# Weights stand still in the output and down projections of an encoder block, and its second norm sums over partitions

## The chip, the cores and the metric

The kernel runs on one core of one Trainium2 chip. Its engines work side by side, each through its own queue in program order: TensorE (PE in the profile, its weight loads PEld), VectorE (DVE), ScalarE (ACT), GpSimd (POOL) and SyncE (SP), which issues most transfers. The metric is the device time of one execution in microseconds (us); all times below are in us unless marked ns.

## The reference

One layer over 1024 tokens of 1024 features, all in float32. What matters here is the part behind the mixers:

```
h = rms_norm(x, norm1_g);  z = h @ w_in          # 1024 x 2560
conv_out = conformer_conv(...)                   # 512 features
attn_out = neighbourhood_attention(...)          # 512 features
mix = concatenate([conv_out, attn_out])          # 1024 x 1024
x = x + mix @ w_out                              # output projection, 1024 x 1024
h = rms_norm(x, norm2_g)                         # mean of squares over the 1024 features
x = x + (silu(h @ w_gate) * (h @ w_up)) @ w_down # 1024 x 2816 twice, then 2816 x 1024
```

`rms_norm` divides each token by the root of the mean square of its features and multiplies by a gain per feature.

## The kernel before

**Products.** Every float32 operand is split into a high part (`hi`, rounded to the matmul's own float32 format) and the rest (`lo`). `mac` (L120) makes one step of a product of three matmuls, hi x hi, hi x lo and lo x hi, each with 128 rows in common, 128 stationary columns and up to 512 moving ones. `split` (L113) makes hi on ACT and lo on DVE or POOL. The three large products (output projection, gate/up, down) are done with seven block products instead of eight, on halves of rows, columns and the common dimension; sums and differences of the halves are the operands. "Half 0" and "half 1" of the tokens are the upper and the lower eight grid rows; each is cut into four column blocks of 128 tokens.

**Attention.** A loop over `i` (L898 to L937) runs 32 head pairs as a pipeline: scores, softmax, transposes of the weights (`flip`), weighted sums (`weigh`). After each block of four pairs `evac_hi` and `evac_lo` (L698 to L719) take the result out of PSUM: half 0 into `rowf`, half 1 into `a11` (hi and lo) and `diff` (half 1 less half 0). The order of the blocks is 0, 3, 1, 2, with half 0 before half 1. Weights of the next stage are split between (`take_parts`).

**Output projection.** The seven groups n1, n7, n4, n6, n5, n2, n3 (L1120 to L1141) each have four accumulators `pb[cb]` and four steps `c` for each. `proj` (L770) holds 128 tokens of the activations still (`lhs`) and moves 512 output features of the weights `wq` past them: the result is 128 tokens by 512 features. `fill` (L869) puts the four steps of n1's block 0 into the end of the attention loop. `read` (L874) adds each result into `x2[t]`, a tile of 128 tokens by 1024 features, on DVE (`put`, L863). Tokens 0 to 3 (half 0) are complete after n5, 4 to 7 (half 1) after n3.

**Second norm.** `norm2(t)` (L943) stores `x2[t]` to `xd` in DRAM for the last residual, sums its squares on ACT along the tile's rows and takes the root; `norm2_out(t)` (L950) scales by the reciprocal and by the gain `g2b`, which lies broadcast over all partitions. Gate/up needs features on partitions, so `turn(t, j)` (L1061) transposes four 128 x 128 blocks on TensorE into PSUM and copies them out with ACT: for half 0 as hi into `h2` and plain into `xT`, for half 1 plain into `xT`. That is 16 calls, 64 transposes.

**Operands of gate/up.** From the two halves `xT` come S1 to S4 (`s_sum`, L1023) and their splits (`s_split`, L1045). A11 and A12 are the parts of `h2`. The first products are m1 and m2 of row blocks 0 to 3, which need A11 and A12 only; then m6 (S2), m5 (S1), m7 (S3), m3 (S4) and m4 (A22), each for blocks 0 and 1, then for 2 and 3. `product` (L1166) runs four steps; `evac` (L1177) reads the bank; `prep` splits the weights four products ahead, on ACT and POOL.

**Order by hand.** All engines' queues follow program order. `weaves` (L1086) fills a list of small jobs, and each step of `proj` or `product` pops one: that puts transposes, norms, splits and conversions between the matmuls. The dictionary `plan` (L1143) does this for products 0 to 14. `x2`, `xn`, `xT`, weights and many others share 22 buffers of one size (`G`); PSUM banks are shared by tag (`mm` four, `tp` two, `cv`).

**Down projection.** `down` (L1358) holds 128 tokens of the hidden activations still and moves 512 features of `w_down`; `finish` adds the residual from `xd`, `store` writes rows of the output.

Of the kernel before, what the change touches and what calls it, by code (L numbers as in the profile page):

```python
# [31 lines left out]
def layout(v):  # L32
# [21 lines left out]
        "x": f["x"],  # L54
        "xt": f["x"].T.reshape(4, 2, P, 2, 512).transpose(3, 0, 2, 1, 4),
# [6 lines left out]
        "g2": f["norm2_g"][None],  # L62
# [12 lines left out]
def build(ctx, tc, a):  # L75
# [622 lines left out]
    def evac_hi(s_):  # L698
        rh, cb = order[s_]
        if rh == 0:  # L700
            if not rowf:
                rowf.extend(G(f"rf{j}").rearrange("p (c b q) -> p c b q", c=2, b=4) for j in range(2))
            for j in range(2):
                act.copy(rowf[j][:, :, cb], os_[s_][:, 2 * j:2 * j + 2])
        else:
            a11[cb] = [w.rearrange("p (c q) -> p c q", c=4) for w in lr(G(f"a11{cb}", F32R))]
            act.copy(a11[cb][0], os_[s_])

    def evac_lo(s_, js=(0, 1)):
        rh, cb = order[s_]  # L710
        if rh == 0:
            return
        if not diff:
            diff.extend(G(f"df{j}").rearrange("p (c b q) -> p c b q", c=2, b=4) for j in range(2))
        for j in js:
            cs = slice(2 * j, 2 * j + 2)
            hi, lo = [w[:, cs] for w in a11[cb]]
            dve.tensor_tensor(lo, os_[s_][:, cs], hi.bitcast(F32), OP.subtract)
            dve.tensor_tensor(diff[j][:, :, cb], os_[s_][:, cs], rowf[j][:, :, cb], OP.subtract)  # L719
# [38 lines left out]
    x2, xn, qop = {}, {}, {}  # L758

    def lhs(p, c, cb):  # L760
        if p == "n1":
            return [w[:, c] for w in a11[cb]]
        q, o = qop[LHS[p]], c * 512 + cb * P
        return [q[:, o:o + P], q[:, 2048 + o:2048 + o + P]]
# [3 lines left out]
    CB = (0, 3, 1, 2)  # L768

    def proj(p, cb, acc, cs=range(4), start=True):  # L770
# [81 lines left out]
    def rows(ap, t):  # L852
        rh, cb = divmod(t, 4)
        return ap.rearrange("(h i w) d -> h i w d", h=2, w=GW)[rh, :, cb * 16:cb * 16 + 16, :]

    def load_x2(t):
        x2[t] = G(f"x2{t}")
        nc.sync.dma_start(x2[t], rows(a["x"], t))

    def add_x(t):  # L860
        return lambda: pool.dma_start(x2[t], rows(a["x"], t), accum_op=OP.add)
# [7 lines left out]
    def fill(*cs):  # L869
        if 0 not in pb:  # L870
            pb[0] = mm("n10")
        proj("n1", 0, pb[0], cs)

    def read(p, cb):  # L874
        acc = pb[cb]
        if p == "n1":
            x2[4 + cb] = G(f"x2{4 + cb}")
            l, r = lr(x2[4 + cb])
            act.copy(l, acc)
            dve.tensor_scalar(r, acc, -1.0, None, op0=OP.mult)  # L880
        elif p == "n7":
            put(cb, 1, acc, OP.subtract)
            put(cb, 0, acc)
        elif p in ("n4", "n6"):
            put(cb, 0, acc, OP.add if p == "n4" else OP.subtract)
        elif p == "n5":
            put(cb, 1, acc)
            put(4 + cb, 1, acc)
            norm2(cb)
        elif p == "n2":  # L890
            put(4 + cb, 0, acc)
        else:
            put(4 + cb, 1, acc)
            norm2(4 + cb)
# [3 lines left out]
    for i in range(2, 32 + 2):  # L898
# [32 lines left out]
        if i > 2:  # L931
# [3 lines left out]
            elif i > 6 and i % 4 in (0, 3):  # L935
                evac_lo((i + 1) // 4 - 2, (0,) if i % 4 == 3 else (1,))
        if jobs:  # L937
            jobs.pop(0)()
    fill(3)

    sd2 = {}

    def norm2(t):  # L943
        nc.sync.dma_start(xd[t * P:(t + 1) * P, :], x2[t])
        ss = SM(f"s2{t}", 1)
        act.activation(cv(f"jk{t}"), x2[t], AF.Square, accum_out=ss)
        sd2[t] = SM(f"r2{t}d", 1)
        act.activation(sd2[t], ss, AF.Sqrt, bias=eps, scale=1.0 / D)

    def norm2_out(t):  # L950
        r = SM(f"r2{t}r", 1)
        dve.reciprocal(r, sd2[t])
        xn[t] = G(f"xn{t}")
        dve.scalar_tensor_tensor(xn[t], x2[t], r, g2b, OP.mult, OP.mult)
# [66 lines left out]
    sn, sop, xT = {}, {}, {}  # L1021

    def s_sum(t, ns, eng):  # L1023
        (x11, x12), (x21, x22) = lr(xT[t]), lr(xT[t + 4])
        for n in ns:
# [3 lines left out]
            if n == 4:  # L1029
                if not s4:  # L1030
                    s4.extend(G(f"s4{j}").rearrange("p (k s) -> p k s", s=512) for j in range(2))
                for j in range(2):
                    eng.tensor_tensor(s4[j][:, :, t * P:(t + 1) * P], *[w[:, j * 256:(j + 1) * 256].rearrange(
                        "p (k s) -> p k s", s=P) for w in (x12, s2)], OP.subtract)
                continue
            o, l, r = ((s1, x21, x22), (s2, x11, s1), (x21, x11, x21))[n - 1]
            eng.tensor_tensor(o, l, r, OP.subtract)

    s4 = []

    def s_rows(n, t):
        return {"S1": lambda: sn[t][:, :512], "S2": lambda: sn[t][:, 512:], "S3": lambda: xT[t + 4][:, :512],
                "A22": lambda: xT[t + 4][:, 512:]}[n]()

    def s_split(n, t, eng=dve):  # L1045
        if n == "S4":
            if t == 0:
                q = [lr(G(f"S4{i}", F32R)) for i in range(HK)]
                sop[n] = [[w[h] for w in q] for h in range(2)]
            split(sop[n][0][t], sop[n][1][t], s4[t // 2][:, t % 2], (eng,))  # L1050
            return
        if n not in sop:
            q = H(n, F32R).rearrange("p (w k s) -> p w k s", w=2, s=512)
            sop[n] = [[q[:, h, i] for i in range(HK)] for h in range(2)]
            sop[n, "all"] = [q[:, h] for h in range(2)]
        split(*[w[:, :, t * P:(t + 1) * P] for w in sop[n, "all"]],
              s_rows(n, t).rearrange("p (k s) -> p k s", s=P), (eng,))

    rest = []

    def turn(t, j):  # L1061
        if not h2:
            h2.extend(H(f"h2{w}", F32R).rearrange("p (k s) -> p k s", s=512) for w in range(2))
        pt = (tp, mm)[j](f"t2{t}{j}")
        for i in range(4):
            kb = 4 * j + i
            pe.transpose(pt[:, i * P:(i + 1) * P], xn[t][:, kb * P:(kb + 1) * P], ident)
        if j == 0:
            xT[t] = G(f"xT{t}")
        w = lr(xT[t])[j]  # L1070
        if t < 4:
            hi, lo = [q[:, 4 * j:4 * j + 4, t * P:(t + 1) * P] for q in h2]
            p3 = pt.rearrange("p (k s) -> p k s", s=P)
            act.copy(hi, p3)
            act.copy(w, pt)
            rest.append(lambda: dve.tensor_tensor(lo, p3, hi.bitcast(F32), OP.subtract))
        else:
            act.copy(w, pt)

    g2b = G("g2b")  # L1080
    nc.sync.dma_start(g2b, a["g2"].to_broadcast([P, D]))
# [16 lines left out]
    def N(t):  # L1098
        return lambda: norm2_out(t)

    def U(t, j):
        return lambda: turn(t, j)
# [7 lines left out]
    lo2 = lambda: rest.pop(0)()  # L1110

    def group(p, cbs=CB):
        for cb in cbs:
            more = p in ("n7", "n5")
            if not more:
                pb[cb] = mm(f"{p}{cb}")
            proj(p, cb, pb[cb], start=not more)
            read(p, cb)

    for cb in CB:  # L1120
        load_x2(cb)
    weaves(12, s0=lambda: (weigh(31), evac_hi(7), evac_lo(7)), s1=QS("Q3", diff, 0, pool), s2=lambda: tails.pop()(), s3=[lambda: read("n1", 0), add],
           s4=QS("Q3", diff, 1, pool), s6=C(0, 1), s10=take)
    group("n1", CB[1:])
# [6 lines left out]
    weaves(16, s1=take, s3=QS("Q4", diff, 1, pool), s6=take, s9=N(0), s13=N(3))  # L1131
# [3 lines left out]
    for _ in range(3):  # L1135
        next_raw()
    weaves(16, s0=take, s1=[N(1), U(0, 0)], s2=U(0, 1), s3=[lo2, lo2], s4=U(3, 0), s5=[U(3, 1), N(2)], s6=[lo2, lo2],
           s7=U(1, 0), s8=U(1, 1), s9=[lo2, lo2, prep], s10=[U(2, 0), take], s11=U(2, 1), s12=[lo2, lo2], s13=prep)
    group("n2")
    weaves(16, s3=prep, s7=prep, s9=N(4), s12=U(4, 0), s13=[U(4, 1), N(7)], s15=SS(0, 1, 2))  # L1140
# [3 lines left out]
        0: dict(s0=U(7, 0), s1=[U(7, 1), N(5)], s3=N(6)),  # L1144
        1: dict(s0=U(5, 0), s1=U(5, 1), s2=SP("S2", 0), s3=SS(3, 1, 2)),
        2: dict(s0=U(6, 0), s1=[U(6, 1), lambda: act.activation(warm, eps, AF.Silu)], s2=SS(1, 1, 2)),
        3: dict(s0=SP("S2", 3), s1=SS(2, 1, 2), s3=SP("S2", 1)),
        4: dict(s0=SP("S2", 2), s1=SP("S1", 0), s3=SP("S1", 3)),
        5: dict(s0=SP("S1", 1), s1=SP("S1", 2), s2=SS(0, 3), s3=SS(3, 3)),
        6: dict(s0=SS(1, 3), s1=SS(2, 3), s3=SP("S3", 0)),  # L1150
        7: dict(s1=SP("S3", 3), s2=SS(0, 4, eng=pool)),
        8: dict(s2=SS(3, 4, eng=pool)),
        9: dict(s1=SP("S3", 1), s3=SS(1, 4)),
        10: dict(s1=SP("S3", 2), s3=SS(2, 4)),
        11: dict(s1=SP("S4", 0), s3=SP("S4", 1)),
# [245 lines left out]
```

## Time and profile before

| what | value |
|---|---|
| median of 3 runs | 1050.73 (1049.7 to 1051.93) |
| the profiled execution, own time | 1050.14 |
| its span, first to last instruction | 1048.4 |
| mean granted TensorE clock | 0.999 of full |
| transposes of `turn`: 64, first and last start | 381.4 and 415.8 |
| first matmul of the gate/up products | 406.38 |
| output of the last block written from | 1041.39 on |

The profile lists instructions by engine with start and length. Matmuls are pipelined: their lengths overlap, so what a matmul costs is its spacing to the next, not its length. A stretch of the trace gives, for each engine, its busy time and its count of instructions; a wait names who ended it.

### The profile page before, as it was taken

To read this page: it belongs to the slowest core of one execution; us is meant where nothing else is said; L and a number is where in the kernel's file an instruction comes from. 1 tells how busy PE (TensorE), PEld (TensorE's weight loads), DVE (VectorE), ACT (ScalarE), POOL (GpSimd) and SP (SyncE) were. 2 spreads that over 40 slices of the span, in tenths; PEclk is the share of its full clock that TensorE was granted. 3 is DMA by queue.
4 is the path that set the end of the run, shared out by engine and by line. 5 is a ranking of instruction groups with operands and counts; after the bars stand their busy time and mean duration, and the time that the engine had idled before them with its cause. 6 is when DMAs were issued, how large, how long until landed. Compare 5 with 4: busy or idle time off the path is not lost.

```text
span 1048.4 us, 13903 instructions
## 1 busy us (share of the span) xinstructions
PE 1028.2 (98%) x4972; PEld 833.8 (80%) x4972; DVE 722.9 (69%) x1097; ACT 465.3 (44%) x915; POOL 452.6 (43%) x342
## 2 busy tenths in 40 slices
PE   7999999999999999999999999999999999999997
PEld 5888888776657888778888888888888888888885
DVE  6768998976896575876564655646556567768883
ACT  6466346636776676532232232232322443443441
POOL 0226578833575863655545454455454100002310
PEclk9999999999999999999999999999999999999999
DMA  9496771285536754465232132232232597633641
GB/s 334 178 271 220 225 238 61 77 244 168 148 109 163 159 182 141 109 167 174 104 131 101 71 131 101 89 132 93 99 111 81 207 326 256 205 101 125 215 133 40
DMA packets 74678, 162.93 MB, mean 155 GB/s; under 512 B 13489, under 2 KB 22193, under 8 KB 73905
## 3 DMA queue, kind: packets, MB, share of 16 engines
q1 hardware_dynamic: 67776, 144.14, 40.7%
q0 software_dynamic: 4864, 10.49, 5.9%
q10 hardware_dynamic: 1968, 7.42, 2.0%
q8 instruction: 39, 0.64, 0.2%
q14 instruction: 31, 0.25, 0.1%
HBM read 122.86 MB, written 53.15 MB: 168 GB/s over the span
## 4 chain that ended last, share of the span: by engine, by line
PE 88%; DVE 4%; POOL 2%; DMA 2%; ACT 2%; issue 2%; SPq 0%; POOLq 0%; ACTq 0%; DVEq 0%
PE B L122 5%; PE B L123 5%; PE B L124 5%; PE D L123 4%; PE D L124 4%; PE D L122 4%; PE A L122 3%; PE A L123 3%; PE A L124 3%; PE z L123 3%; PE z L122 3%; PE z L124 3%; PE gl L124 3%; PE gl L123 3%; PE gl L122 3%; PE n L122 3%
## 5 line engine op out<-in xcount | busy, mean ns | idle before, releaser
L347 DVE SCALAR_TENSOR_TENSOR cv<-u,par,cv 128x1009 f32<-128x1009 f32 (+14 forms) x85 | 108.5, 1276 | 2.0
L373 POOL TENSOR_TENSOR pa<-pa,pr 128x1022 f32<-128x1022 f32 (+10 forms) x31 | 75.2, 2426 | 33.7 <-ACT pr L372 32.2
L1356 POOL TENSOR_TENSOR ou<-ou,resm 128x512 f32<-128x512 f32 x8 | 12.5, 1571 | 142.5 <-DMA resm<-xd 142.5
L114 ACT CAST op<-sr 128x512 fp32r<-128x512 f32 x77 | 47.7, 619 | 52.7 <-PE B2d L124 21.3
L118 DVE TENSOR_TENSOR op<-sr,op 128x512 fp32r<-128x512 f32 x77 | 58.2, 756 | 16.4 <-ACT op L114 16.4
L1193 DVE TENSOR_TENSOR g<-B,g 128x512 f32<-128x512 f32 x22 | 15.2, 690 | 71.3 <-PE B L124 68.2
L1202 ACT ACTIVATE D<-D 128x512 f32<-128x512 f32 x22 | 12.8, 582 | 112.5 <-DVE D L1201 112.5
L1185 DVE TENSOR_TENSOR u<-B,g 128x512 f32<-128x512 f32 x22 | 15.2, 691 | 61.0 <-PE B L124 61.0
L668 POOL TENSOR_SCALAR e<-e,rs 128x288 f32<-128x288 f32 (+1 forms) x64 | 35.0, 568 | 45.6 <-DVE rs L666 41.0
L114 ACT CAST op<-wd 128x512 fp32r<-128x512 f32 x66 | 40.9, 620 | 30.4 <-DVE wd L1280 17.4
L118 DVE TENSOR_TENSOR op<-wd,op 128x512 fp32r<-128x512 f32 x66 | 50.5, 765 | 1.9 <-ACT op L114 0.3
L986 DVE TENSOR_TENSOR ts<-ts,gu 128x512 f32<-128x512 f32 x36 | 43.3, 1203 | 0.6
L1191 ACT ACTIVATE A<-A 128x512 f32<-128x512 f32 x18 | 10.5, 582 | 68.6 <-PE A L124 68.6
L661 ACT ACTIVATE e<-e,mx 128x288 f32<-128x288 f32 (+1 forms) x64 | 36.3, 569 | 2.9 <-DVE mx L659 2.8
L659 DVE CUSTOM_DVE_ANT_0 e<-s,tab 128x288 f32<-128x288 f32 (+1 forms) x64 | 29.7, 501 | 8.7 <-PE s L646 8.4
L372 ACT ACTIVATE pr<-u,par 128x1022 f32<-128x1022 f32 (+10 forms) x31 | 34.2, 1135 | 1.2 <-ACT vs L433 1.2
L677 PEld LDWEIGHTS p<-ident,e 128*96 128x96 f32 (+1 forms) x192 | 20.0, 133 | 18.1 <-POOL e L668 10.4
L677 PE MATMUL p<-ident,e 128*96 128x128 f32 (+1 forms) x192 | 28.5, 281 | 2.3 <-DVE pT L682 1.0
L986 DVE TENSOR_TENSOR ts<-gu 128x512 f32<-128x512 f32 x18 | 30.1, 1670 | 0.0
L865 DVE TENSOR_TENSOR x<-x,n 128x512 f32<-128x512 f32 x32 | 21.0, 681 | 13.1 <-PE n L124 13.1
L693 PE MATMUL o<-pT,vw 96*64 96x128 f32 (+1 forms) x384 | 28.0, 281 | 0.0
L646 PE MATMUL s<-kT,qT 64*128 64x288 f32 (+1 forms) x128 | 26.7, 495 | 0.0
(1066 smaller groups left out, 3524.1 us busy)
## 6 DMA issues: line engine op xcount, KB each, us to landing
sr<-sd SPq DMA_DIRECT2D x77, 256.0 KB
gu<-in_gu SPq DMA_DIRECT2D x36, 512.0 KB
sd<-sd SPq DMA_DIRECT2D x22, 512.0 KB
wd<-in_wd SPq DMA_DIRECT2D x44, 256.0 KB
sd<-g SPq DMA_DIRECT2D x33, 256.0 KB
x<-in_x SPq DMA_DIRECT2D x12, 512.0 KB
xd<-x SPq DMA_DIRECT2D x8, 512.0 KB
resm<-xd SPq DMA_DIRECT2D x16, 256.0 KB
```

The lines of the kernel that those rows point to most:

```text
L114: act.copy(hi, src)
L118: eng.tensor_tensor(*[w[..., sl] for w in (lo, src, hi.bitcast(F32))], OP.subtract)
L122: pe.matmul(acc, lh, rh, start=start, stop=False, skip_group_check=True)
L123: pe.matmul(acc, lh, rl, start=False, stop=False, skip_group_check=True)
L124: pe.matmul(acc, ll, rh, start=False, stop=stop, skip_group_check=True)
L347: dve.scalar_tensor_tensor(acc[:, o], uc[:, i], dwk[:, c, t:t + 1], acc[:, o], OP.mult, OP.add)
L372: act.activation(pr[:, o], uc[:, i], AF.Copy, scale=dwk[:, c, t:t + 1])
L373: pool.tensor_tensor(pa[:, o], pa[:, o], pr[:, o], OP.add)
L661: act.activation(e[:, hh], e[:, hh], AF.Exp, bias=mx, scale=-1.0, accum_out=rs[:, hh:hh + 1])
L668: pool.tensor_scalar(es[i][:, hh], es[i][:, hh], rs[:, hh:hh + 1], 1.0, op0=OP.mult, op1=OP.mult)
L677: pe.transpose(pt[:m, g * P:(g + 1) * P], es[i][:, hh, g * m:(g + 1) * m], ident)
L986: dve.tensor_tensor(lr(tsum[i, 1])[n - 3] if o is None else o, l, r, OP.add)
```

## The change

In the output projection and in the down projection the two operands of each matmul change places. The weights' 128 columns stand still and 512 tokens move. Results lie as 128 features by 512 tokens. `x2[t]` now means a half of the tokens (`t // 4`) and feature blocks: 128 features of block `t % 4` for the left half of the features, beside those for the right half. The input is given a second time in this order (`x2`), and the output is written in it and put back in order by the host.

The second norm sums over partitions. Each tile's squares are made by ACT and added up by DVE; a product with a column of ones (`token_sums`) gives each token's sum, 128 tokens on partitions; after the root and the reciprocal, `token_rows` transposes a broadcast of each column, so that a PSUM tile holds every token's factor in all partitions; `scale2` multiplies `x2` in place by the gain (now a column per feature block) and this tile. `turn` is gone.

`a11` is laid out by feature pairs over all tokens; the first block of half 1 is kept plain (`early`) and split at steps 20 and 22 of the attention loop. n1's first two accumulators are made in parts, since the last token block is not ready when they begin.

```
+    def early_split(j):
+        hi, lo = [a11[w, j][:, :, 0] for w in range(2)]
+        split(hi, lo, early[0][:, 2 * j:2 * j + 2], (dve,))
...
+    JB, EARLY, LATE, FULL = range(4), (slice(0, 256), slice(384, 512)), (slice(256, 384),), (slice(0, 512),)
+
+    def proj(p, jb, acc, cs=range(4), start=True, parts=FULL, woven=True):
         w = wq[RHS[p]]
         for c in cs:
-            mac(acc, lhs(p, c, cb), [w[:, o + c * 512:o + c * 512 + 512] for o in (0, 2048)],
-                start and c == 0, c == 3)
-            weave()
+            for sl in parts:
+                mac(acc[:, sl], [w[:, o + c * 512 + jb * P:o + c * 512 + jb * P + P] for o in (0, 2048)],
+                    [q[:, sl] for q in right(p, c)], start and c == 0 and sl.start == 0, c == 3)
+            if woven:
+                weave()
...
+    def squares(t):
         nc.sync.dma_start(xd[t * P:(t + 1) * P, :], x2[t])
+        h, jb = divmod(t, 4)
+        sq = G(f"sq{t}")
+        act.activation(sq, x2[t], AF.Square)
+        if sqs.get((h, "last")):
+            sqs.pop((h, "last"))()
+        if jb == 0:
+            sqs[h] = sq
+            return
+        sqs[h, "last"] = lambda: dve.tensor_tensor(sqs[h], sqs[h], sq, OP.add)
+        if jb == 3:
+            sqs.pop((h, "last"))()
+            l, r = lr(sqs[h])
+            dve.tensor_tensor(l, l, r, OP.add)
+
+    def token_sums(h):
+        pt = tp(f"ss{h}")
+        for k in range(4):
+            pe.matmul(pt[:, k:k + 1], sqs[h][:, k * P:(k + 1) * P], one, start=True, stop=True)
+        sd = SM(f"r2{h}d", 4)
+        act.activation(sd, pt[:, :4], AF.Sqrt, bias=eps, scale=1.0 / D)
+        rt[h] = SM(f"r2{h}r", 4)
+        dve.reciprocal(rt[h], sd)
+
+    def token_rows(h):
+        rw[h] = tp(f"rw{h}")
+        for k in range(4):
+            pe.transpose(rw[h][:, k * P:(k + 1) * P], rt[h][:, k:k + 1].to_broadcast([P, P]), ident)
+
+    def scale2(h, jb, d):
+        w = lr(x2[4 * h + jb])[d]
+        dve.scalar_tensor_tensor(w, w, g2[:, 4 * d + jb:4 * d + jb + 1], rw[h], OP.mult, OP.mult)
+        return w
...
+    def left2(jb, d):
+        w = scale2(0, jb, d)
+        hi, lo = [q[:, 4 * d + jb] for q in h2]
+        act.copy(hi, w)
+        if rest:
+            rest.pop()()
+        rest.append(lambda: dve.tensor_tensor(lo, w, hi.bitcast(F32), OP.subtract))
...
+    pb[1] = mm("n11")
+    proj("n1", 1, pb[1], parts=EARLY)
+    for jb in range(2):
+        proj("n1", jb, pb[jb], parts=LATE, woven=False)
+        read("n1", jb)
...
+    weaves(16, s0=take, s7=TS(0), s9=[TR(0), prep], s10=[A(0, 0), take], s11=A(1, 0), s12=A(2, 0), s13=[A(3, 0), prep], s15=A(0, 1))
     group("n2")
+    weaves(16, s1=A(1, 1), s3=prep, s4=A(2, 1), s7=[A(3, 1), lambda: rest.pop()(), prep])
     group("n3")
...
+        1: dict(s3=TS(1)),
+        2: dict(s1=[TR(1), lambda: act.activation(warm, eps, AF.Silu)], s2=X(0, 1, 2)),
+        3: dict(s1=X(1, 1, 2)),
+        4: dict(s0=SP("S2", 0, pool), s1=X(2, 1, 2)),
+        5: dict(s0=SP("S2", 1, pool), s1=X(3, 1, 2)),
+        6: dict(s0=SP("S2", 2), s1=SP("S2", 3), s2=SP("S1", 0), s3=SP("S1", 1)),
+        7: dict(s1=SP("S1", 2), s3=SP("S1", 3)),
+        8: dict(s1=SS(0, 3), s2=SS(1, 3), s3=SS(0, 4, eng=pool)),
+        9: dict(s1=SS(2, 3), s2=SS(3, 3), s3=SS(1, 4, eng=pool)),
+        10: dict(s1=SP("S3", 0), s3=[SP("S3", 1), SS(2, 4, eng=pool)]),
+        11: dict(s1=SP("S3", 2), s2=SP("S3", 3), s3=SS(3, 4, eng=pool)),
+        12: dict(s1=SP("S4", 0), s3=SP("S4", 1)),
+        13: dict(s1=SP("S4", 2), s3=SP("S4", 3)),
+        14: dict(s1=SP("A22", 0), s3=SP("A22", 1)),
+        15: dict(s1=SP("A22", 2), s3=SP("A22", 3)),
...
     def down(n, t):
-        mac(acc, [q[:, h, t * P:(t + 1) * P] for h in range(2)], [q[:, 2 + h] for h in range(2)],
+        mac(acc, [q[:, 2 + h, t * P:(t + 1) * P] for h in range(2)], [q[:, h] for h in range(2)],
```

`TS`, `TR` and `A` put `token_sums`, `token_rows` and `left2` at a step; `X(jb, 1, 2)` scales both halves of a tile of half 1 and makes its parts of S1 and S2; `SS` and `SP` are the other sums and splits, on DVE unless `pool` is named. A split of an operand now covers all 512 tokens of one step k, where it covered 128 tokens of all four steps. `product`, `evac` and `prep` are unchanged.

More of the change, by code (lines that the diff above doesn't have):

```diff
@@ L699, in evac_hi @@
         rh, cb = order[s_]
[L700 to L707, printed above, removed]
+        if rh == 0 and not rowf:
+            rowf.extend(G(f"rf{j}").rearrange("p (c b q) -> p c b q", c=2, b=4) for j in range(2))
+        if s_ == 1:
+            early.append(ST("early").rearrange("p (c q) -> p c q", c=4))
+            act.copy(early[0], os_[s_])
+            return
+        if rh == 1 and not a11:
+            a11.update({(w, j): G(f"a11{w}{j}", F32R).rearrange("p (c b q) -> p c b q", c=2, b=4)
+                        for w in range(2) for j in range(2)})
+        for j in range(2):
+            act.copy((a11[0, j] if rh else rowf[j])[:, :, cb], os_[s_][:, 2 * j:2 * j + 2])
+    early = []
+    def early_split(j):
+        hi, lo = [a11[w, j][:, :, 0] for w in range(2)]
+        split(hi, lo, early[0][:, 2 * j:2 * j + 2], (dve,))
     def evac_lo(s_, js=(0, 1)):
@@ L939, in build @@
     fill(3)
[L941 to L954, printed above, removed]
+    rt, rw = {}, {}
+    g2, one = par[:, 32:40], par[:, 40:41]
+    nc.sync.dma_start(g2, a["g2"])
+    dve.memset(one, 1.0)
+    def squares(t):
+        nc.sync.dma_start(xd[t * P:(t + 1) * P, :], x2[t])
+        h, jb = divmod(t, 4)
[5 more added lines that the diff above has]
+            sqs[h] = sq
+            return
+        sqs[h, "last"] = lambda: dve.tensor_tensor(sqs[h], sqs[h], sq, OP.add)
[19 more added lines that the diff above has]
+        return w
     HK, QF = KB // 2, FB // 2
@@ L1020, in build @@
     h2 = []
-    sn, sop, xT = {}, {}, {}
+    sn, sop = {}, {}
     def s_sum(t, ns, eng):
-        (x11, x12), (x21, x22) = lr(xT[t]), lr(xT[t + 4])
+        (x11, x12), (x21, x22) = lr(x2[t]), lr(x2[t + 4])
         for n in ns:
@@ L1028, in s_sum @@
             s1, s2 = lr(sn[t])
[L1029 to L1036, printed above, removed]
+            o, l, r = ((s1, x21, x22), (s2, x11, s1), (x21, x11, x21), (x12, x12, s2))[n - 1]
@@ L1059, in build @@
-    rest = []
-    def turn(t, j):
+            else:
+                q = H(n, F32R).rearrange("p (w k s) -> p w k s", w=2, s=512)
+                sop[n] = [[q[:, h, i] for i in range(HK)] for h in range(2)]
+        split(sop[n][0][t], sop[n][1][t], s_rows(n, t), (eng,))
+    def left2(jb, d):
         if not h2:
             h2.extend(H(f"h2{w}", F32R).rearrange("p (k s) -> p k s", s=512) for w in range(2))
[L1064 to L1078, printed above, removed]
@@ L1096, in C, with A, TS, X @@
         return lambda: conv_silu(h, c)
[L1098 to L1102, printed above, removed]
+    def A(jb, d):
+        return lambda: left2(jb, d)
+    def TS(h):
+        return lambda: token_sums(h)
+    def X(jb, *ns):
+        def f():
+            scale2(1, jb, 0)
+            scale2(1, jb, 1)
+            s_sum(jb, ns, dve)
+        return f
+    def TR(h):
+        return lambda: token_rows(h)
     def SS(t, *ns, eng=dve):
@@ L1108, in SP, with group @@
         return lambda: s_split(n, t, eng)
-    lo2 = lambda: rest.pop(0)()
-    def group(p, cbs=CB):
-        for cb in cbs:
+    def group(p):
+        for jb in JB:
             more = p in ("n7", "n5")
             if not more:
[L1116 to L1122, printed above, removed]
-           s4=QS("Q3", diff, 1, pool), s6=C(0, 1), s10=take)
-    group("n1", CB[1:])
+                pb[jb] = mm(f"{p}{jb}")
+            proj(p, jb, pb[jb], start=not more)
+            read(p, jb)
+    for jb in JB:
+        load_x2(jb)
+    weaves(12, s0=lambda: (weigh(31), evac_hi(7), evac_lo(7)), s1=QS("Q3", diff, 0, pool), s2=lambda: tails.pop()(), s3=add,
+           s4=QS("Q3", diff, 1, pool), s6=C(0, 1), s10=take)
+    pb[1] = mm("n11")
[3 more added lines that the diff above has]
+        read("n1", jb)
+    for jb in (2, 3):
+        pb[jb] = mm(f"n1{jb}")
+        proj("n1", jb, pb[jb])
+        read("n1", jb)
     weaves(16, s1=C(0, 2), s5=take, s9=C(0, 3), s11=add_x(4), s13=QS("Q2", diff, 0, pool))
@@ L1130, in build @@
     group("n6")
-    weaves(16, s1=take, s3=QS("Q4", diff, 1, pool), s6=take, s9=N(0), s13=N(3))
+    weaves(16, s1=take, s3=QS("Q4", diff, 1, pool), s6=take)
     group("n5")
```

106 lines of the change are left out of this document (38 added, 68 removed).

## The prediction, made before the changed kernel was run

> **What bounds the kernel now.** First the page: shares of the engines, and the chain of work that ended last.
>
> ```profile
> span 1048.4 us, 13903 instructions
> PE 1028.2 (98%) x4972; PEld 833.8 (80%) x4972; DVE 722.9 (69%) x1097; ACT 465.3 (44%) x915; POOL 452.6 (43%) x342
> PE 88%; DVE 4%; POOL 2%; DMA 2%; ACT 2%; issue 2%; SPq 0%; POOLq 0%; ACTq 0%; DVEq 0%
> ```
>
> TensorE is the bound over the whole span. So each instruction taken from it is worth its spacing, except where it waits. The stretches (busy time of PE, PEld, DVE, ACT, POOL, each with its count) say where that is:
>
> ```profile
> 380.00:406.40 26.40, 26.40 (x138) 21.97 (x137) 17.96 (x27) 18.67 (x36) 9.95 (x7) 1.00 0.56 184
> 414.20:456.10 41.90, 39.74 (x176) 31.64 (x174) 36.59 (x41) 24.32 (x45) 26.56 (x21) 1.00 0.41 114
> 456.10:1041.40 585.30, 585.20 (x2579) 483.89 (x2579) 370.37 (x488) 193.38 (x348) 204.96 (x149) 1.00 0.40 138
> ```
>
> From 380 to 406 (n2, n3) TensorE never rests; after 456 neither. Between, while the gate/up operands S1 to S4 and A22 are made, it loses 2.2, and VectorE is busy for 36.6 of 41.9. The waits of TensorE there:
>
> ```profile
> PE B L122 <- DVE u L1185: 1.4, 1, 1.4
> PE D L123 <- DVE A L118: 0.4, 1, 0.4
> PE B L123 <- DVE S L118: 0.3, 1, 0.3
> ```
>
> All three end with VectorE. In this stage VectorE, with GpSimd beside it, is nearly as tight as TensorE.
>
> **The change, part by part.** I sum against the profiled execution (span 1048.4, 1050.14 in all, 0.6 below the median of 1050.73) and put the difference on the median. The projections keep their products; only the operand that stands still changes, and both operands are 128 rows by 128 or 512 columns as before, so I cost that swap at nothing, as long as the weight load (0.11, below) hides under a 512-wide matmul (0.227). TensorE's order of time gives the prices:
>
> ```profile
> 380.01 0.39 PE L122 MATMUL n<-wB,A 128*128 128x512 f32 x1
> 380.69 0.39 PE L122 MATMUL n<-wB,A 128*128 128x512 f32 x1
> 384.34 0.60 PE L1067 MATMUL t<-ident,xn 128*128 128x128 f32 x4
> 384.69 0.48 PE L122 MATMUL n<-wB,A 128*128 128x512 f32 x1
> 385.47 0.60 PE L1067 MATMUL t<-ident,xn 128*128 128x128 f32 x4
> 406.38 0.39 PE L122 MATMUL A<-h,t0m 128*128 128x512 f32 x1
> 455.34 0.39 PE L122 MATMUL D<-A,t0m 128*128 128x512 f32 x1
> 456.13 0.50 PE L123 MATMUL D<-A,t0m 128*128 128x512 f32 x1 [0.39 <-DVE A L118]
> ```
>
> One step of a product is three matmuls and takes 0.68; with four transposes ahead 1.13. So a group of four costs 0.45, though each is shown as 0.27 long.
>
> *Transposes dropped:* 64, in 16 groups: -7.2. `token_rows` adds two groups: +0.9.
>
> The page's row of `weigh`, then TensorE's order of time and that of its weight loads:
>
> ```profile
> L693 PE MATMUL o<-pT,vw 96*64 96x128 f32 (+1 forms) x384 | 28.0, 281 | 0.0
> 315.97 0.55 PE L677 MATMUL p<-ident,e 128*128 128x128 f32 x3
> 316.45 0.88 PE L693 MATMUL o<-pT,vw 128*64 128x128 f32 x12
> 317.25 0.19 PEld L122 LDWEIGHTS n<-wB,a 128*128 128x128 f32 x1 [0.17 <-issue]
> 317.36 0.19 PEld L123 LDWEIGHTS n<-wB,a 128*128 128x128 f32 x1
> ```
>
> *`token_sums`:* eight products with one moving column. Such plain f32 products run as two instructions each (384 for 192 calls in `weigh`). Twelve take 0.80, 0.067 each, with half-width weights; two full weight loads follow each other at 0.11. 16 x 0.11 = +1.8 (ends 1.1 and 2.6).
>
> *Narrow matmuls:* n1 for jb 0 and 1 is cut at the token blocks that are ready: 24 matmuls of 512 columns become 24 of 256 and 48 of 128. The columns are equal, so the lower end is 0. If each waits for its weight load, 0.11 + 0.11 + 0.12 against 0.227 is +2.7; that is the value I take, since the loads' own spacing is the nearest row. Upper end 5.
>
> VectorE's last subtraction for a11, and TensorE's first matmul after `weigh(31)`:
>
> ```profile
> 326.90 0.42 DVE L718 TENSOR_TENSOR a<-o,a 128x256 fp32r<-128x256 f32 x1
> 325.49 0.50 PE L122 MATMUL n<-wB,a 128*128 128x512 f32 x1
> ```
>
> The late parts need the last token block: `weigh(31)`, then two ACT copies and two subtractions. Those took until 327.3 before, 1.8 after `weigh(31)`'s last matmul (325.5); three early steps of about 0.68 lie between. I cost it at nothing; without that cover up to 1.8.
>
> VectorE in steps 20 to 22 of the attention loop, without a gap between these two rows:
>
> ```profile
> 288.82 0.42 DVE L718 TENSOR_TENSOR a<-o,a 128x256 fp32r<-128x256 f32 x1
> ...
> 293.85 0.17 DVE L666 RECIPROCAL rs<-rs 128x2 f32<-128x2 f32 x1 [0.56 <-ACT e L661]
> ```
>
> *Attention:* two subtractions of 0.42 move from steps 11 and 12 to 20 and 22, with an ACT copy each, and three of the four a11 copies become two of half width. The first shifts the loop, the second falls before a gap of 0.56: +0.4, ends 0 and 1.6.
>
> The page's row of the Square, and a 1024-wide operation of VectorE:
>
> ```profile
> L946 ACT ACTIVATE jk<-x 128x1024 f32<-128x1024 f32 x8 | 8.2, 1027 | 11.2 <-DVE x L865 11.2
> 409.88 1.29 DVE L954 SCALAR_TENSOR_TENSOR xn<-x,r26r,g2b 128x1024 f32<-128x1024 f32 x1
> ```
>
> *Ahead of `token_sums(1)`* stand, after n3's last product, an addition from PSUM, the Square, a 1024-wide addition and a 512-wide one. 0.68 + 1.03 + 1.29 + 0.68 is 3.7, some 4 with handing over, and two products (5.44) cover it. It is late only if VectorE's queue is: 24 operations of 0.6, four long additions of 1.2 and about 5 lost to GpSimd fill 24 of the 26 of n2 and n3. Nothing is taken, up to 1.
>
> ACT's table loads, and the root and reciprocal of the old norm:
>
> ```profile
> 53.01 1.28 ACT L480 ACT_TABLE_LOAD   x1 [0.31 <-DVE sg L479]
> 373.94 1.28 ACT L948 ACT_TABLE_LOAD   x1
> 375.24 0.29 ACT L948 ACTIVATE r20d<-s,eps 128x1 f32<-128x1 f32 x1
> 375.97 0.16 DVE L952 RECIPROCAL r20r<-r20d 128x1 f32<-128x1 f32 x1
> ```
>
> *A wait in n2:* `token_rows(0)` stands two steps (1.36) behind `token_sums(0)`, and between them ACT takes a square root and VectorE a reciprocal, with a table load that here waits for its input (0.31 at L480). 1.28 + 0.29 + 0.16 and some 0.4 of handing over is 2.1, less 1.36: +0.8, ends 0 (load early) and 2. The next matmuls of n2 queue behind it. For the second half the table is still loaded: 0.8 in 1.36, no wait. [...]
>
> Without waits in the operand stage: -7.2 + 0.9 + 1.8 + 2.7 + 0.4 + 0.8 = **-0.6**.
>
> The last three xd stores, and a transfer of the same size with its time to landing:
>
> ```profile
> 402.09 6.40 SPq L944 DMA_DIRECT2D xd<-x  x3
> x<-in_x POOLq DMA_DIRECT2D x4, 512.0 KB, 11.0
> ```
>
> *Other moved work.* In n5 to n3, ACT loses accumulator reads, PSUM copies and most square roots; VectorE loses eight 1024-wide scalings, gains six 1024-wide additions, and stays below TensorE. Scaling in place must now wait until the xd store has read x2. The last store goes out by 408.5; even the 11 of a POOL transfer of that size ends at 419.5, and x2 7 is scaled last, after 423. SP's g2 load shrinks. Output stores keep 2 KB pieces. The down projection keeps its counts. All cost nothing; a late xd would delay the queue below one for one.
>
> *The operand stage.* The second half's norm starts only when n3 is complete. n3 ends at 406.38 - 10 x 0.45 + 0.9 + 0.45 + 2.7 + 0.4 + 0.8 = 407.1; two products (5.44), sums (0.9), two steps (1.36) and rows (0.45) put the first scaling at 415.4. From there VectorE has 46 operations up to the last A22 split: 16 for X, 2 S2, 4 S1, 4 + 4 S3, 4 S4, 4 A22, 8 evacuations. GpSimd has 20: 14 weight splits, 2 S2 splits, 4 S4 sums. In the old stretch: 41 (four half wide), and 14 with four half wide (the 21 counts three DMA issues).
>
> ```profile
> 338.79 2.48 DVE L865 TENSOR_TENSOR x<-x,n 128x512 f32<-128x512 f32 x4
> 443.16 5.14 DVE L118 TENSOR_TENSOR S<-s,S 128x512 fp32r<-128x512 f32 x2
> 442.92 1.74 POOL L118 TENSOR_TENSOR t1m<-gum,t1m 128x512 fp32r<-128x512 f32 x1
> 444.18 1.73 POOL L118 TENSOR_TENSOR t0m<-gum,t0m 128x512 fp32r<-128x512 f32 x1
> 445.42 1.73 POOL L118 TENSOR_TENSOR t1m<-gum,t1m 128x512 fp32r<-128x512 f32 x1
> L865 DVE TENSOR_TENSOR x<-x,n 128x512 f32<-128x512 f32 x32 | 21.0, 681 | 13.1 <-PE n L124 13.1
> ```
>
> Undisturbed, four take 2.48, so 0.60 each; beside three GpSimd operations two took 5.14. The old 41 would take 23.6 undisturbed, but were busy for 36.6: 13.0 extra over some 16 GpSimd operations, 0.8 each. Operations that read PSUM stay at 0.68 (L865, 32 of them, mean 681 in the page), and their share doubles (7 of 41 to 15 of 46), so I reduce the extra: 20 x 0.8 x 0.81 = 13.0.
>
> 46 x 0.60 + 13.0 + 1.5 idle (5.3 before, most of it waiting for ACT and transposed tiles) = 42.1: the last split ends at 457.5. A split is now whole per k, so product 16 (the first D<-A) may start 2.0 before it, at 455.5. Unstalled it would start at 407.1 + 0.9 + 0.45 + 16 x 2.72 = 452.0, so 3.5 are lost. Before: 455.34 and 0.56 of waiting inside, 455.9, against 406.38 + 6 x 0.45 + 43.5 = 452.6 unstalled: 3.3 lost (more than the 2.2 of idle time, since the first matmul after a pause is slower). The end thus moves by 455.5 - 455.9 = **-0.4**; after product 16 TensorE is gapless in both. 1050.73 - 0.4 = **1050.3**.
>
> **The rivals.** That the change doesn't do what it says is none: the transposes are gone from the code. *The operand stage doesn't bind.* If GpSimd's blocking falls mostly into VectorE's PSUM reads and only 0.7 is lost, the result is -0.6 - 3.3 + 0.7 = -3.2: 1047.5. For: ACT is relieved, strided splits become contiguous, idle time shrinks. Against: 36.6 busy of 41.9 already. With narrow matmuls free as well, 1044.8. It counts as faster once the last split ends before 455.8.
>
> *VectorE and GpSimd take turns (the slower side).* Place: the 46 operations from 415.4 on. Without my reduction and with half the old idle time: 27.6 + 16.0 + 2.7 = 46.3, last split 461.7, product 16 at 459.7: +3.8, 1054.5. It decides from a last split at 460 on. For: the 5.14 row, and six full operations on GpSimd where four halves stood, with the weight splits queued behind them. Against: eight of the 16 operations of X read PSUM.
>
> [...]
>
> *No gain because the narrow matmuls and sums cost their upper ends:* +3.1 before product 16 moves the first scaling as well: 1053.4. For: three f32 transposes of 128 columns took 0.16 each (315.97 to 316.45). Against: four took 0.09 each (384.34 to 384.69).
>
> **How the numbers follow.** Forecast 1050.3, its own range 1048.6 to 1052.8, which is the 0.2% (2.1) that a measurement can tell from no change. Chances: forecast 0.42; stage doesn't bind 0.33; taking turns or upper ends, 0.25. So faster 0.33, same 0.42, slower 0.25. The range takes in most of both sides, 1046.3 to 1054.0.
>
> **What would show it.** Right: L1067 gone; n1 with 128- and 256-wide matmuls at about 0.11 spacing; a wait near 0.8 at `token_rows(0)`; VectorE gapless from about 415 to 457; product 16 near 455.5. Wrong: the last A22 split before 455.8 or after 460; narrow matmuls near 0.06; waits in n3 or in the attention steps 18 to 26; a wait on the xd store; matmuls of the down projection off 0.227.

## The result, and the profile after

The changed kernel takes 1058.48 (median of 5 runs, 1056.9 to 1059.25), the kernel before 1050.57 beside it: a ratio of 1.0073, 95% interval 1.0059 to 1.0088. It is slower by 7.9; 1050.3 was predicted, with a range up to 1054.0.

The page of the changed kernel: span, engines and the chain that ended last.

```profile
span 1056.3 us, 13879 instructions
PE 1030.9 (98%) x4980; PEld 837.2 (79%) x4980; DVE 737.0 (70%) x1102; ACT 456.4 (43%) x890; POOL 456.8 (43%) x344
PE 86%; DVE 7%; issue 2%; ACT 2%; DMA 1%; POOL 1%; SPq 0%; POOLq 0%; DVEq 0%; ACTq 0%
```

VectorE's share of the chain has gone from 4% to 7%. The stretches (busy time of PE, PEld, DVE, ACT, POOL, each with its count, then the granted clock, the DMA share and GB/s), with the borders at the starts of products 0 and 16 moved along with the program and 380 and 414.2 left where they were:

```profile
380.00:407.10 27.10, 25.82 (x121) 21.23 (x120) 24.97 (x31) 13.46 (x19) 11.97 (x7) 1.00 0.43 153
414.20:466.60 52.40, 44.79 (x181) 36.22 (x182) 47.27 (x47) 24.44 (x45) 32.08 (x24) 0.90 0.35 100
466.60:1052.20 585.60, 585.57 (x2581) 483.87 (x2579) 368.82 (x487) 192.96 (x348) 203.45 (x148) 1.00 0.40 138
```

The last row is the old one: 2581 matmuls in 585.60, before 2579 in 585.30. The loss is in the middle row: the operand stage lasts 52.4 where it lasted 41.9, and the granted clock in it is 0.90. The waits of TensorE from 320 to 500 (total, count, longest; `ss` is the tile of `token_sums`, `B` is the PSUM bank of m6, m5 and m3, `D` that of m7 and m4):

```profile
PE D L124 <- DVE S L119: 4.0, 1, 4.0
PE B L123 <- ACT t1m L115: 3.3, 1, 3.3
PE ss L976 <- DVE sq L971: 3.1, 2, 1.8
```

TensorE's order of time shows what each wait costs (start, length, and at the end the wait before it):

```profile
407.07 0.39 PE L123 MATMUL A<-h,t0m 128*128 128x512 f32 x1
...
414.47 1.02 PE L976 MATMUL ss<-par,sq 128*128 128x1 f32 x8 [1.80 <-DVE sq L971]
...
442.75 0.47 PE L123 MATMUL B<-S,t0m 128*128 128x512 f32 x1 [3.30 <-ACT t1m L115]
...
454.36 0.79 PE L124 MATMUL D<-S,t0m 128*128 128x512 f32 x1 [4.04 <-DVE S L119]
454.95 0.63 PE L125 MATMUL D<-S,t0m 128*128 128x512 f32 x1
455.38 0.63 PE L123 MATMUL D<-S,t0m 128*128 128x512 f32 x1
455.80 0.63 PE L124 MATMUL D<-S,t0m 128*128 128x512 f32 x1
...
466.57 0.39 PE L123 MATMUL D<-A,t0m 128*128 128x512 f32 x1
```

Behind the wait of 4.04 matmuls stand 0.43 apart instead of 0.227; the granted clock from 454.3 to 457.5 is 0.51. Product 0 begins at 407.07, 0.7 later than before (407.1 was predicted); product 16 at 466.57, against 455.9 before with its wait: 10.7 later. Only 7.9 reach the end. From TensorE's last matmul to the end of the span it was 7.4 (1040.96 to 1048.4) and is 4.5 (1051.80 to 1056.3).

Why the operands are late, in VectorE's and then GpSimd's order of time:

```profile
412.69 1.64 DVE L971 TENSOR_TENSOR sq<-sq 128x512 f32<-128x512 f32 x1
...
418.22 1.41 DVE L989 SCALAR_TENSOR_TENSOR x<-x,par,rw 128x512 f32<-128x512 f32 x2 [2.21 <-PE rw L985]
...
424.12 1.40 DVE L989 SCALAR_TENSOR_TENSOR x<-x,par,rw 128x512 f32<-128x512 f32 x2
...
430.95 2.46 DVE L1066 TENSOR_TENSOR sn<-x,sn 128x512 f32<-128x512 f32 x1
...
441.92 0.68 DVE L1211 TENSOR_TENSOR u<-B,g 128x512 f32<-128x512 f32 x1
...
446.22 8.68 DVE L119 TENSOR_TENSOR S<-x,S 128x512 fp32r<-128x512 f32 x2
...
465.39 3.48 DVE L119 TENSOR_TENSOR A<-x,A 128x512 fp32r<-128x512 f32 x2
```

```profile
424.35 1.30 POOL L119 TENSOR_TENSOR t3m<-gu3None,t3m 128x512 fp32r<-128x512 f32 x1 [1.42 <-ACT t3m L115]
...
431.11 1.75 POOL L119 TENSOR_TENSOR t1m<-gum,t1m 128x512 fp32r<-128x512 f32 x1
...
445.88 1.74 POOL L119 TENSOR_TENSOR t1m<-gum,t1m 128x512 fp32r<-128x512 f32 x1
447.13 1.73 POOL L1066 TENSOR_TENSOR x<-x,sn 128x512 f32<-128x512 f32 x1
448.38 1.72 POOL L119 TENSOR_TENSOR t0m<-gum,t0m 128x512 fp32r<-128x512 f32 x1
...
452.09 1.66 POOL L119 TENSOR_TENSOR t0m<-gum,t0m 128x512 fp32r<-128x512 f32 x1
```

The first row is the last addition of the squares, on which the wait of 1.80 ends. Two S3 splits, 1.2 of work, last 8.68 while GpSimd runs six operations without a gap, 1.25 apart. Two scalings that read PSUM (424.12) keep their 0.70 each beside a GpSimd operation; an addition with both inputs in SBUF (430.95) takes 2.46. From the first scaling to the end of the last A22 split it is 50.7 (418.22 to 468.87): 46 operations of 0.6 are 27.6, and the other 23 fall on 20 GpSimd operations, 1.15 each. That puts all of the rest down to GpSimd; 1.4 of it is idle time of VectorE. The 31 operations with both inputs in SBUF are lengthened, beyond the 0.68 of an undisturbed one, by 20.0 in all: 1.0 for each GpSimd operation.

### The profile page after: what moved, and what is told of

It reads as the page before. It is cut to its first block, busy times and chain, and to the rows that moved or that the text cites. A ratio compares the mean times of both kernels' runs of the same rounds, so it can differ in the third digit from the quotient of the medians.

```text
span 1056.3 us, 13879 instructions
## 1 busy us (share of the span) xinstructions
PE 1030.9 (98%) x4980; PEld 837.2 (79%) x4980; DVE 737.0 (70%) x1102; ACT 456.4 (43%) x890; POOL 456.8 (43%) x344
## 4 chain that ended last, share of the span: by engine, by line
PE 86%; DVE 7%; issue 2%; ACT 2%; DMA 1%; POOL 1%; SPq 0%; POOLq 0%; DVEq 0%; ACTq 0%
PE B L125 5%; PE B L124 5%; PE B L123 5%; PE D L124 4%; PE D L125 4%; PE D L123 4%; PE A L125 3%; PE A L124 3%; PE A L123 3%; PE z L123 3%; PE z L124 3%; PE z L125 3%; PE gl L125 3%; PE gl L123 3%; PE gl L124 3%
## 5 line engine op out<-in xcount | busy, mean ns | idle before, releaser
L678 PEld LDWEIGHTS p<-ident,e 128*96 128x96 f32 (+1 forms) x192 | 19.9, 133 | 18.4 <-POOL e L669 10.7
```

The costliest lines, as they stand in the source:

```text
L678: pe.transpose(pt[:m, g * P:(g + 1) * P], es[i][:, hh, g * m:(g + 1) * m], ident)
```

## Experiments

Theory G: GpSimd's operations stop VectorE for nearly their whole length (1.0 to 1.15 each by the counts above, where they start 1.25 apart), and this makes the operand stage late. Rivals: V, VectorE's queue is too long in any case; P, the late sums and the pauses at them carry the loss on.

**S4 sums off GpSimd (e1), and left out (e2)**

```
-        8: dict(s1=SS(0, 3), s2=SS(1, 3), s3=SS(0, 4, eng=pool)),
+        8: dict(s1=SS(0, 3), s2=SS(1, 3), s3=SS(0, 4)),
...
```

(the same for the other three; in the second kernel the four are taken out)

> The changed kernel with the four S4 sums on VectorE in place of GpSimd. Theory G (GpSimd's unbroken run of weight splits and S4 sums from 439.7 to 453.8 stretches VectorE's S3 splits to 8.68 and holds ScalarE's weight casts): the pair of splits falls to about 2.5, the 4.04 wait of TensorE goes and the 3.30 one shrinks; 1058.5 falls by 5 to 8, to 1051 to 1053.5. Rival V (VectorE's queue from the first scaling on is too long, whatever GpSimd does): four more operations of 0.69 lengthen it, and product 16 starts about 2.7 later: 1061.

> The changed kernel without the S4 sums on any engine (S4's splits take the right half of x2 as it is, so that the output is another). Theory G: as good as the kernel with the sums on VectorE, better by at most 2.7 (their own length), so 1050 to 1053. Rival V: VectorE's queue has the same operations as in the changed kernel; within 1.5 of 1058.5.

Measured: 1055.60 (ratio 1.005, 1.0033 to 1.0067) and 1055.06 (1.0046, 1.0031 to 1.0061). Four more operations on VectorE made the kernel 2.9 faster, so V falls; but G's 5 to 8 was too much. The queues say why: from first scaling to last split 48.2 (418.68 to 466.87) and 45.7 (420.41 to 466.11). Four operations moved give 2.5, against 4 x (1.15 - 0.6) = 2.2 by G; four left out give 4.9, against 4.6. Of the wait of 4.04 in bank D only 0.9 and 0.6 are left, but 4.7 and 3.3 stand in bank B, and in both a slow stretch (matmuls 0.43 apart) fell into n2, and product 0 began 1.9 and 2.2 later.

**The sums of squares: less to wait for (e3), or later (e4)**

```
-            l, r = lr(sqs[h])
-            dve.tensor_tensor(l, l, r, OP.add)
...
+            for d in range(2):
+                pe.matmul(pt[:, k:k + 1], sqs[h][:, d * 512 + k * P:d * 512 + (k + 1) * P], one, start=d == 0, stop=d == 1)
```

and, in another kernel (which in n2 moves `TS(0)` and `TR(0)` by two steps as well):

```
...
-        1: dict(s3=TS(1)),
-        2: dict(s1=[TR(1), lambda: act.activation(warm, eps, AF.Silu)], s2=X(0, 1, 2)),
-        3: dict(s1=X(1, 1, 2)),
+        2: dict(s2=TS(1)),
+        3: dict(s0=[TR(1), lambda: act.activation(warm, eps, AF.Silu)], s1=X(0, 1, 2), s3=X(1, 1, 2)),
```

> The changed kernel without the last 512-wide addition of the squares; token_sums takes eight products for each half instead of four, added up in PSUM. TensorE works 0.9 more for each half, and the addition of 2.76 and the one of 1.64, on which the two waits (1.28 and 1.80) end, are gone. Theory P (the waits at the sums, the half-clock stretch of some 3 us behind the second, and the late first scaling carry a part of the loss on): waits gone, first scaling near 416, total down by 2 to 4, to 1054.5 to 1056.5. Rival L (only the late stalls at products 10 and 12 count, and they are set by GpSimd's queue): the gain ahead is used up in those waits, 1057.5 to 1059.5.

> The changed kernel with token_sums and token_rows two steps later in n2 and three steps later in the first gate/up products (2.04 us); nothing else is moved but the scalings behind them. Theory P: both waits go and with them the slow stretch behind the second; the first scaling is at about 416.3 in place of 418.2: total down by 2 to 4.9. Rival L: 1057.5 to 1059.5, as before.

Measured: 1057.24 (1.0065, 1.005 to 1.008) and 1059.22 (1.0084, 1.0069 to 1.0099). The waits at the sums went to nothing and to 0.3, and the first scaling came at 417.28 and 417.10 instead of 418.22. But the queue behind it lasted 50.7 and 52.5, and TensorE waited 4.1 + 2.8 and 4.7 + 2.3 + 2.2 there. The 2 to 4.9 of theory P are not there: e3 is 1.2 below the changed kernel, about the 0.9 by which its queue started earlier, and e4 0.7 above it, with a queue 1.8 longer; both differences are within the spread of the runs. (e3 lies 0.3 below L's range too.) So P doesn't explain the loss: product 16 starts where the queue's start and length put it, at 466.07 and 467.31 against 466.57.

**What a pause costs (e5)**

```
+        if p == "m1" and i >= 6 and i % 2 == 0:
+            q = sop["A11"][0][0]
+            for _ in range((1, 1, 2, 2, 4, 4, 8, 8)[i // 2 - 3]):
+                dve.tensor_scalar(q, q.bitcast(F32), 1.0, None, op0=OP.mult)
```

> The kernel before, with 1, 1, 2, 2, 4, 4, 8, 8 in-place multiplications by one (VectorE, on a block of A11 that the next matmul reads) ahead of the first product of gate/up row blocks 6, 8, ... 20, where TensorE is otherwise gapless. Each makes TensorE wait: some 1.5 to 4.5 us by count. Theory C (a pause costs more than it lasts, since the granted clock falls for some us behind it, as behind the waits of 1.80, 3.30 and 4.04 in the changed kernel): behind the longer pauses matmuls stand 0.43 apart instead of 0.227 for 2 to 3.5 us, an extra 1 to 2 for each. Rival: matmuls are back at 0.227 within three of them, extra under 0.3 each, and the total grows by the sum of the pauses.

Measured: 1085.85 (one run). TensorE's order of time behind the third and the fifth pause:

```profile
607.82 0.47 PE L122 MATMUL A<-h,t10m 128*128 128x512 f32 x1 [1.67 <-DVE h L1302]
608.13 0.40 PE L123 MATMUL A<-h,t10m 128*128 128x512 f32 x1
608.36 0.39 PE L124 MATMUL A<-h,t10m 128*128 128x512 f32 x1
...
689.80 0.77 PE L122 MATMUL A<-h,t14m 128*128 128x512 f32 x1 [3.64 <-DVE h L1302]
690.36 0.63 PE L123 MATMUL A<-h,t14m 128*128 128x512 f32 x1
690.79 0.63 PE L124 MATMUL A<-h,t14m 128*128 128x512 f32 x1
691.22 0.63 PE L122 MATMUL A<-h,t14m 128*128 128x512 f32 x1
```

| pause beyond the spacing | extra behind it |
|---|---|
| 1.37, 1.36, 1.82, 1.82 | 0.10, 0.11, 0.08, 0.08 |
| 3.80, 3.80, 5.64, 5.65 | 2.85, 2.70, 1.72, 2.80 |

(the extra is what the next 25 spacings take beyond 0.227 each). Up to 1.8 the rival is right, from 3.8 on theory C, with 1.7 to 2.9 where 1 to 2 was expected: seven to thirteen matmuls stand 0.43 apart. Pauses and extras add up to 35.7, and the time grew by 35.5 (1050.39 to 1085.85). Over the whole span the granted clock was 0.986, against 0.998 to 0.999 in the kernel before. Where between 1.82 and 3.80 the extra sets in, these pauses don't show. The waits of 3.30 and 4.04 in the changed kernel each had such a stretch, at a granted clock of 0.50 (443.9 to 447.2) and 0.51 (454.3 to 457.5): product 10 took 4.37 (442.75 to 447.12) instead of 2.72, product 12 lost 1.7 besides its wait. The wait of 1.80 had one too (0.52 from 416.7 to 420.0), where the eight one-column products of `token_sums` (0.9) followed it; why it had one, and the pauses of 1.82 here none, is not shown.

**The narrow matmuls once more (e6)**

```
-            proj(p, jb, pb[jb], start=not more)
+            proj(p, jb, pb[jb], start=not more, parts=EARLY + LATE if p == "n4" and jb < 2 else FULL)
```

> The changed kernel with n4's first two feature blocks cut as n1's are (24 matmuls of 512 columns become 24 of 256 and 48 of 128). If a 128-wide matmul costs its weight load (0.11), n4 to n3 come 2.7 later and the whole is 2.7 longer, 1061.2; if columns alone count, 1058.5. Should the time behind n3 be set by something other than TensorE, the shift would show in n4 and be lost behind: also 1058.5.

Measured: 1062.57 (1.0114, 1.0099 to 1.013), 4.1 more than the changed kernel. n4 takes 14.49 (348.24 to 362.73), against 11.85 there (347.83 to 359.68): +2.64. Its 72 narrow matmuls, 256 or 128 columns wide, mostly stand 0.11 to 0.12 apart, as n1's do in the changed kernel, where their weight loads are 0.11 apart. In the profile of this kernel a slow stretch of 1.4 followed the sums in n2 (`token_rows` started at 395.65 with 0.18 between transposes), where the profile of the changed kernel has none. It has the size of the other 1.4 of the medians, but that it is in most of the runs is not shown.

**GpSimd out of the stage (e7), and less of it in the kernel before (e8)**

```
-            split(*top[i, p], src, (pool,))
+            split(*top[i, p], src, (dve if 5 <= n_prep[1] <= 20 else pool,))
```

(in the first kernel with the two S2 splits and the four S4 sums on VectorE too; in the second this line alone, in the kernel before)

> The changed kernel with GpSimd's part of the operand stage (weight splits of products 5 to 20, two S2 splits, four S4 sums) on VectorE. Theory G in its strict form (VectorE stands still for nearly the whole of each GpSimd operation: 50.7 from the first scaling to the last A22 split are 46 x 0.6 = 27.6 and 23 for 20 GpSimd operations, 1.15 each): the queue becomes 66 x 0.6 = 39.6 and some 1.5 idle, the last A22 split comes 8 to 10 earlier, total 1049 to 1052. Rival V: VectorE gets 20 more operations of 0.69 and the stage becomes longer by up to 13.8: 1062 or more.

> The kernel before with the weight splits of products 5 to 20 on VectorE in place of GpSimd. Strict theory G: VectorE gains more than it takes on, and up to 3.3 of lost TensorE time go: 1047.5 to 1050. Rival V: 16 more operations of 0.69 in a stage where VectorE is busy for 36.6 of 41.9 make it late: 1054 or more.

Measured: 1048.53 (0.9987, 0.9977 to 0.9997) and 1047.88 (0.9977, 0.9966 to 0.9988). The changed kernel gains 9.9 from giving VectorE 22 more operations. Its stage without GpSimd, then the first scaling and the last A22 splits:

```profile
414.20:457.00 42.80, 40.90 (x177) 33.41 (x178) 40.77 (x67) 24.45 (x45) 2.44 (x2) 0.96 0.45 123
```

```profile
416.62 1.41 DVE L989 SCALAR_TENSOR_TENSOR x<-x,par,rw 128x512 f32<-128x512 f32 x2
...
456.36 1.29 DVE L119 TENSOR_TENSOR A<-x,A 128x512 fp32r<-128x512 f32 x2
```

67 operations of VectorE instead of 47 in that stretch, and less time: 41.0 from first scaling to last split (416.62 to 457.65), where 41.1 was expected; the total came 0.5 below the range, as the first scaling was 1.6 earlier too. G is shown. The queue is 9.6 shorter with the 20 GpSimd operations moved into it, 0.48 each, so by this an operation of 0.6 cost VectorE 1.08 when GpSimd did it. The kernel before gains 2.5 by the edit of the weight splits alone: product 16 starts at 453.11, and TensorE's wait for u, 1.4 before, is the only one left from 380 to 475:

```profile
PE B L122 <- DVE u L1185: 0.8, 1, 0.8
```

**Product 10 (e10), and the sums later with it (e11)**

In the changed kernel the wait of 3.30 is put down to ScalarE's t1m. But product 10 adds to the bank that `u`, the evacuation of product 8 (441.92, ends 442.60), must have read, and it starts at 442.75. The edit of e10, against the kernel of e7:

```
-        8: dict(s1=SS(0, 3), s2=SS(1, 3), s3=SS(0, 4)),
-        9: dict(s1=SS(2, 3), s2=SS(3, 3), s3=SS(1, 4)),
+        9: dict(s0=SS(0, 3), s1=SS(1, 3), s2=[SS(2, 3), SS(0, 4)], s3=[SS(3, 3), SS(1, 4)]),
```

> The changed kernel with GpSimd out of the operand stage (as in e7), and two S3 sums and one S4 sum moved from product 8 to product 9, behind the evacuation of product 8 (u = B less g). Theory U (product 10 waits for that evacuation, which stands in VectorE's queue behind the S3 sums; the profile names ScalarE's t1m because it ended at nearly the same time): the wait of 1.90 ahead of product 10 goes, 1046.5 to 1047.5. Rival B (it is the cast of t1m, whose buffer comes free with the first S4 sum): that sum is now later by some 2, the wait grows to 3 or more, 1049.5 to 1051.

> As e10, with token_sums and token_rows of the first half two steps later in n2 and of the second half one step later. By theory G and U the waits at the sums (1.28 and 0.85) go too, and the second half's scaling starts no later: 1044.5 to 1046.0. If, as in e4, the stage's queue only waits in another place, 1046.5 to 1048.

Measured: 1048.88 (0.9985, 0.9977 to 0.9994) and 1048.18 (0.9975, 0.9965 to 0.9985); neither is faster than e7 by more than the spread. In e10 the wait ahead of product 10 is gone, as U has it:

```profile
438.07 0.47 PE L123 MATMUL B<-S,t0m 128*128 128x512 f32 x1
...
442.88 0.62 PE L123 MATMUL B<-S,t1m 128*128 128x512 f32 x1 [1.83 <-DVE u L1210]
```

The same wait now stands ahead of product 11, whose evacuation is queued behind the six sums put into product 9. Of product 10's wait U was right; of the total it was wrong, and so was the 1044.5 to 1046.0 for e11. In e11 the waits at the sums fell to 0.7, product 0 began at 406.10, and product 16 at 456.91, as in e7 (456.94): the queue (41.0 again) sets it.

**The tail (e9), and the fastest version (e12)**

```
         (nc.scalar if p == "m4" else nc.sync).dma_start(
-            rows(a["out"], 4 * tok + t)[:, :, d * 512:(d + 1) * 512], w)
+            a["out"][tok, t][:, d * 512:(d + 1) * 512], w)
...
```

> The kernel before, its output written tile by tile (128 tokens in a row of DRAM addresses) and put in order by the host; nothing else. From the last matmul to the end of the span the kernel before takes 7.4, the changed one 4.5. Theory D (the place of the rows in DRAM sets how fast the last stores go): the tail shrinks by 2 to 3, 1047.5 to 1048.5. Rival: the tail's 2.9 comes from something else of the change (the last steps of the down projection), and the total stays at 1050.4.

> The kernel before with both: weight splits of products 5 to 20 on VectorE (e8, 1047.9) and the output tile by tile (e9). Theory D: the two add up, 1045 to 1046. Rival: 1047.5 to 1048.5.

Measured: 1047.49 (0.9969, 0.9958 to 0.9981) and 1044.97 (0.9948, 0.9935 to 0.996). The tail is 4.5 (1041.66 to 1046.2), and the two edits add up. The last four stores, transfers from 1036 to 1060 in 40 slices (busy share in tenths, then packets), in the kernel before and in e9:

```profile
DMA  0000025355455454520000000000000000000000
...
DMA packets 544, 1.05 MB, mean 44 GB/s; under 512 B 32, under 2 KB 32, under 8 KB 544
```

```profile
DMA  0000009173462900000000000000000000000000
...
DMA packets 576, 1.05 MB, mean 44 GB/s; under 512 B 64, under 2 KB 64, under 8 KB 576
```

With rows taken from eight grid rows of 16 tokens the engines' share never passes 0.5; with 128 rows evenly apart it reaches 0.9. The small packets double, 8 for each store to 16. An estimate from these shares is that the stores went over 8 of the 16 engines before and over all in e9; no view here shows which engines carried them. e12, the old layout with both edits, beats both kernels: 5.4 less than before. Its nearest partner is e11, which has the new layout, the weight splits on VectorE and the output by tiles: 1048.18, with product 16 at 456.91 where e12 has 453.39. So with the output's order in both and GpSimd's weight splits out of both, the new layout is still 3.2 slower.

## Why the prediction was wrong, point by point

- **Swapped operands at nothing:** right. Matmuls keep 0.227, n7 to n5 take 46.42 in both kernels, and the down projection keeps its density.
- **Transposes out, rows in:** right. From n2's start to product 0 it is 24.66 (382.41 to 407.07) against 26.37 before; -4.5 for ten groups, +0.9 for the sums, +0.35 for the rows and a wait of 1.28 give -2.0, and -1.7 was measured.
- **Narrow matmuls +2.7:** right: 2.70 more from n1's first matmul behind `weigh(31)` to n7, and 2.64 in e6.
- **Attention +0.4:** not seen. The first matmul behind `weigh(31)` starts at 325.19, before at 325.49.
- **The wait at `token_rows(0)`, +0.8:** wrong in place. Nothing waited there, as the table load ran at 385.35, before the sums. Instead `token_sums(0)` waited 1.28 for VectorE's last addition, which the prediction leaves out. That product 0 came out where predicted is partly luck: attention was 0.7 less, and n2 and n3 0.6 more, than in the sum.
- **`token_sums(1)`, "Nothing is taken, up to 1":** wrong. It waited 1.80. VectorE's additions of squares (1.23 to 1.28 each) and the 512-wide one (1.64) were queued behind each other until 414.3, and with the slow stretch that followed the first scaling came at 418.22, not 415.4 (the terms named for it add up to 415.3): 2.8 of the loss.
- **The operand stage, 46 x 0.60 + 13.0 + 1.5 idle = 42.1:** the mechanism was named, the term of 13.0 for GpSimd was mis-sized, and this is the step that failed. I took 0.8 for each GpSimd operation from the old stretch, where 3.0 of VectorE's 5.3 idle lay beside GpSimd operations and so did not stretch it, and multiplied it by 0.81. Measured are 20.0 of lengthening, and 23 with the idle time and the small losses, 1.0 to 1.15 each: 50.7 in all. With 2.8 and 8.6 the last split comes 11.4 after the 457.5 forecast, product 16 11.1 after 455.5. The rival *take turns* had the mechanism, but with the same 0.8: 46.3. The 1.0 to 1.15 measured are most of the 1.25 from one GpSimd operation to the next. As the reduction by 0.81 assumes, operations that read PSUM weren't stretched (0.70 each at 424.12, beside a GpSimd operation), but only 8 of the 15 stood beside one, and 1.4 of idle time comes on top.
- **Pauses cost their length:** wrong, and not in the sum. Unstalled, product 16 would start at 407.07 + 0.9 + 0.45 + 43.5 = 451.9, so 14.7 were lost and not 3.5. Of these 9.1 are waits (1.80, 3.30, 4.04); most of the other 5.5 are three slow stretches of about 1.7 each.
- **"Output stores keep 2 KB pieces ... cost nothing":** wrong on the other side: -2.9 at the end. So +11.1 - 2.9 = +8.2 on 1050.3, which is the 1058.5 measured.
- **The rival *stage doesn't bind*** at 0.33 was the farthest off, and no rival came near: the slowest, *take turns*, ended at 1054.5.

## What to carry to other kernels

Where VectorE is the tight engine, price GpSimd's help at what it takes from VectorE: a sum or split over SBUF that VectorE does in 0.6 cost it 1.0 to 1.15 here when GpSimd did it. A gain on TensorE ahead of a stage that a queue sets was worth little here until that queue was shorter, so count the queue's start and length first; sums over the partitions start it only when the whole half of the tokens is complete. Price a pause of TensorE by its length as well: between the dense matmuls of e5, one of up to 1.8 cost 0.1 more than it lasted, one of 3.8 or 5.6 cost 1.7 to 2.9 more.

## What was not expected

The output's order in DRAM was worth 2.9 in the kernel before (7.4 to 4.5 behind the last matmul); the changed kernel, which has that order, also takes 4.5. ScalarE's load of the square root's table did not wait for the root's input: it started at 385.35, the root at 390.35. The wait of 1.2 to 1.3 at `token_sums(0)` was followed by a slow stretch of about 1.5 in the profiles of e1, e2, e6 and e10 and by none in those of the changed kernel and e7; in e11 even the 0.73 at `token_sums(1)` was followed by one. With full matmuls behind it, the wait of 1.83 ahead of product 11 had eight of them 0.42 to 0.43 apart in e10 and none in e11. So a short pause went either way here, and what decides stays open. And the engine named at a wait was wrong once: ScalarE's t1m ended at 442.62, 0.02 after the evacuation of product 8, which e10 shows to be the cause in the kernel without GpSimd.
